# Experts' input rows fetched from DRAM by indirect DMA instead of being selected by matmuls

## The chip, the cores and the metric

The kernel runs on one core of one Trainium2 chip. The metric is the device time of one execution in microseconds (us). The core has TensorE (PE; its weight loads are listed apart as PEld), VectorE (DVE), ScalarE (ACT), GpSimd (POOL) and SyncE (SP), which issues nearly all transfers; 16 DMA engines carry them. "L0" and "L1" below are the two layers of the model, "L312" and the like are lines of the kernel.

## What is computed

Two layers over 256 latent tokens and, in the first layer, 256 context tokens, of width 1024 in float32. Each layer has a mixer and then a mixture of 32 experts; each token goes to the two best experts of its best group. The mixers don't change here. The expert part, cut down:

```python
def hier_moe(h, wg_r, bg_r, we_r, be_r, w_gate, w_up, w_down):   # h: (T, 1024), T = 512 in L0, 256 in L1
    pg = softmax(h @ wg_r + bg_r); pg_top, g_idx = top_k(pg, 1)             # 4 groups
    le = take_along_axis((h @ we_r + be_r).reshape(t, 4, 8), g_idx)         # 8 experts of the group
    pe_top, e_local = top_k(softmax(le), 2)
    wts = pg_top * pe_top / sum(pe_top)
    ...                                                                     # sort tokens by expert into blocks
    xs = h[slot_tok]                                                        # a row per slot
    ys = (silu(xs @ w_gate[e]) * (xs @ w_up[e])) @ w_down[e]                # 1024x512, 1024x512, 512x1024
    return segment_sum(ys * slot_w, slot_tok)
```

## The kernel before, in words

**Stages.** The program runs the L0 mixer, the L0 output projection with the router, the L0 experts, the L1 mixer, the L1 projection with the router, and the L1 experts. A scheduler orders the instructions of each engine by priority and by a model of time; inside `moe` the order on PE is the order in which the code is written (`manual_schedule`).

**Router.** `out_proj` ends with x_sb, the residual rows, 128 tokens a tile (NT = 4 tiles in L0, 2 in L1). `done` then calls, for each tile, `ffn_logits` (transposes, 36 logits), `route_tile` (DVE: ranks and the selection `selb`; PE counts over it) and `ffn_split`, which makes the expert input `h2` as a high part `h2h` and a low part `h2l` (ACT, DVE and POOL), all kept in SBUF. `route_end` turns the counts into `pos`, the place of each token among its expert's slots.

**Experts.** Each expert has CAP = 64 slots; two experts make a unit (u0 to u15 a layer, and in L0 one more, uX, of a single expert, for tokens above 64: `extra_block`, between u2 and u3). For a group of four experts `group` makes `gt`, a 0/1 matrix of tokens by slots (DVE, L435), and `gather` multiplies `h2h` and `h2l` with it (L265): the transposed input rows `xT` of 256 slots, 8 chunks of 128 features, NT tiles, two parts each. On PE a step of the loop over units is

- `hidden(0)`: first expert, 8 chunks of gate (L312) and up (L313) products, with hooks after given chunks (scatters of the units before, `places`);
- of the unit before: `turn` (L331), four transposes of its hidden layer, which DVE copies (`aT`, L333), a block of the gather for the next group, and `down` (L347), the product with w_down, then `yh`, `yl` on ACT and DVE or POOL;
- a second block of the gather, with the weights per slot (L285) in every second step;
- `hidden(1)`: the second expert, with hooks.

`scatter` (L370, L371) adds a unit's weighted result to the tokens' rows: PE multiplies (`sc`), DVE scales (`tm`, L375), DVE and POOL add (`x_sb`, L376). Each chunk-3 and chunk-7 hook holds one. In u0 the gather for the second group stands between the two experts, and the gather of uX stands between `turn` and `down` of u1.

**Weights.** An expert's weights are 6 tiles of 1 MiB; SP issues the loads in the order in which units use them (`moe_weights`), each into the next of a ring of tiles: NW = 5 named w and NX = 5 (L0) or 9 (L1) named wx. A load waits until its tile's last reader is done. The w tiles come free during the projection, the wx tiles lie where the projection's buffers were and can be loaded when it ends. A gate or up load reads 4 rows, 8 KB in a row, for each partition; a down load reads two rows of 4 KB that lie apart (`"(c p) f -> p c f"`, L153).

Of the kernel before, what the change touches and what calls it, by code (L numbers as in the profile page):

```python
# [25 lines left out]
I32 = mybir.dt.int32  # L26
U8 = mybir.dt.uint8
# [5 lines left out]
D = 1024  # L33
# [5 lines left out]
NX = (5, 9)  # L39
NZ = (0, 0)  # L40
EXTRA = 3
HP = 300
# [16 lines left out]
class Trunk:  # L59
# [13 lines left out]
    def consts(self, pool):  # L73
# [175 lines left out]
    def gather(self, NT, h2h, h2l, gt, ne):  # L249

        nc = self.nc
        N = ne * CAP
        if ne == 1:
            xT = self.mp.tile([128, 8, CAP], F32, name="xT1")
        else:
            xT = self.mp.tile([128, 8, GRP * CAP], F32, name="xT", bufs=2)
        per = 512 // N

        def part(c0):
            ps = self.mps.tile([128, 512], F32, name="xg", bufs=1).rearrange("p (k n) -> p k n", k=per)  # L260
            for k in range(per):
                i = 0
                for t in range(NT):
                    for src in (h2h, h2l):
                        nc.tensor.matmul(ps[:, k], src[:, t, c0 + k, :], gt[t], start=(i == 0), stop=(i == 2 * NT - 1))  # L265
                        i += 1
            if self.slot_mods is None:
                nc.scalar.activation(xT[:, c0:c0 + per, :], ps, AF.Copy)
            else:
                A, B = self.slot_mods  # L270
                for k in range(per):
                    c = c0 + k
                    nc.vector.tensor_scalar(xT[:, c], ps[:, k], A[:, 0, c:c + 1], B[:, 0, c:c + 1], op0=OP.mult, op1=OP.add)  # L273

        return xT, [lambda c0=c0: part(c0) for c0 in range(0, 8, per)]

    def slot_weights(self, NT, gt, whl, M, cols):

        nc = self.nc
        R = whl.shape[2]  # L280
        n = len(cols)
        pw = self.mps.tile([128, 512], F32, name="mx", bufs=1).rearrange("p (n r) -> p n r", r=64)
        for i in range(n):
            for t in range(NT):
                nc.tensor.matmul(pw[:M, i, 0:R], gt[t][:, i * M:(i + 1) * M], whl[:, t, :], start=(t == 0), stop=(t == NT - 1))  # L285
        wl = self.mp.tile([128, 2, 64], F32, name="wl", bufs=2)
        nc.vector.tensor_copy(wl[:M, 0:n, 0:R], pw[:M, 0:n, 0:R])
        ws = self.mp.tile([128, 2], F32, name="ws", bufs=3)
        for i in range(n):
            for j, (a, b) in enumerate(cols[i]):  # L290
                r = slice(64 * j, 64 * j + 64)
                nc.vector.tensor_add(ws[r, i:i + 1], wl[r, i, a:a + 1], wl[r, i, b:b + 1])
        return [ws[:, i:i + 1] for i in range(n)]

    def unit(self, W, xT, slots, ws, posbc, NT, x_sb, mx5, last=False):
# [92 lines left out]
    def slot_mx5(self, S, mx5):  # L388
# [4 lines left out]
        m = self.mp.tile([128, 8, GRP * CAP], F32, name="xT", bufs=2)  # L393
        m = m.rearrange("p c n -> p (c n)")[:, :D]
# [29 lines left out]
    def moe(self, l, NT, h2h, h2l, pos, whl, counts, weights, first, posT, x_sb, mx5, early):  # L424
# [1713 lines left out]
```

## Time and profile before

| | |
|---|---|
| runs (3), median | 1825.58 us (1823.93 to 1826.13) |
| the profiled execution, its own time | 1826.54 us |
| its span, first to last instruction | 1824.5 us |
| busy, share of the span | PE 93%, PEld 54%, DVE 47%, ACT 24%, POOL 20% |
| HBM read over the span | 508.09 MB, 280 GB/s on average |

The share of busy time says little here: PE is listed as busy over 90% in both expert stages, and a matmul's end is modelled. The stages are read apart: the first gate product of L0 starts at 444.8 us, the last scatter ends at 999.8 us; in L1 it is 1348.1 us and the end of the span.

### The profile page before, as it was taken

What the parts mean: (1) busy time and instruction counts of PE and PEld (TensorE: products, weight loads), DVE (VectorE), ACT (ScalarE), POOL (GpSimd) and SP (SyncE); (2) the same over time, 40 slices, a digit from 0 to 9 for tenths busy, and PEclk for the clock granted to TensorE, in tenths of its full rate; (3) what the DMA queues carried; (4) which work ended last, traced back from release to release, by engine and by line L of the source; (5) the groups of instructions that cost most, each with busy time, mean ns of one, the idle gap of its engine ahead of it and who ended that gap; (6) DMA issues with size and microseconds to landing.
All of it is one profiled execution on the core that took longest, in us unless ns stands there. A gap on an engine that the chain in (4) does not pass through costs nothing. (4 is left out here: it accounts for less than half of the span.)

```text
span 1824.5 us, 22067 instructions
## 1 busy us (share of the span) xinstructions
PE 1693.6 (93%) x8722; PEld 982.8 (54%) x8722; DVE 856.5 (47%) x1624; ACT 430.2 (24%) x692; POOL 357.6 (20%) x315
## 2 busy tenths in 40 slices
PE   6999988987999999999988998899879999999997
PEld 4766677775454444444433776588643334434442
DVE  3336158776234434344344678776443332333222
ACT  2335244432101110111101654443410000000000
POOL 2102055232011212112122300232310110101010
PEclk9999999987989999999998899899969999999999
DMA  8655530334978999999995335600479999999996
GB/s 295 236 213 210 211 124 25 119 98 165 373 322 322 395 385 400 396 395 401 392 387 194 122 110 198 228 31 1 155 290 415 415 417 416 416 416 417 416 416 282
DMA packets 115674, 511.79 MB, mean 281 GB/s; under 512 B 16254, under 2 KB 26434, under 8 KB 77031
## 3 DMA queue, kind: packets, MB, share of 16 engines
q1 hardware_dynamic: 115564, 510.31, 71.4%
q8 instruction: 71, 1.16, 0.3%
q14 instruction: 39, 0.32, 0.0%
HBM read 508.09 MB, written 2.18 MB: 280 GB/s over the span
## 5 line engine op out<-in xcount | busy, mean ns | idle before, releaser
L313 PE MATMUL gu<-wx,xT 128*64 128x512 f32 x640 | 292.2, 600 | 1.3 <-DMA wx<-moe_w_up_in 1.0
L312 PE MATMUL gu<-w,xT 128*64 128x512 f32 x568 | 262.0, 603 | 0.0
L312 PE MATMUL gu<-wx,xT 128*64 128x512 f32 x472 | 215.9, 599 | 0.0
L347 PE MATMUL y<-wx,aT 128*64 128x512 f32 x648 | 179.9, 615 | 12.1 <-DVE aT L333 9.0
L313 PE MATMUL gu<-w,xT 128*64 128x512 f32 x400 | 183.2, 602 | 0.5 <-SPq L599 0.5
L376 POOL TENSOR_TENSOR x_sb<-x_sb,tm 128x512 f32<-128x512 f32 x64 | 98.9, 1546 | 390.1 <-DVE tm L375 390.1
L316 ACT ACTIVATE sg<-gu 64x512 f32<-64x512 f32 x65 | 38.5, 592 | 555.6 <-PE gu L313 555.6
L375 DVE TENSOR_TENSOR tm<-sc,mx 128x512 f32<-128x512 f32 x128 | 85.5, 688 | 155.5 <-PE sc L371 153.8
L312 PEld LDWEIGHTS gu<-w,xT 128*64 128x64 f32 x568 | 72.5, 138 | 121.6 <-issue 118.1
L347 PE MATMUL y<-w,aT 128*64 128x512 f32 x392 | 120.1, 610 | 10.2 <-DVE aT L333 7.6
L265 PE MATMUL xg<-gt,h2h 128*128 128x256 f32 (+1 forms) x416 | 116.6, 314 | 10.3 <-DVE xT L273 6.0
L121 DVE TENSOR_TENSOR wl<-w,wh 128x1024 fp32r<-128x1024 f32 (+1 forms) x62 | 80.0, 1290 | 93.3 <-ACT wh L120 92.5
L265 PE MATMUL xg<-gt,h2l 128*128 128x256 f32 (+1 forms) x416 | 109.9, 297 | 0.0
L313 PEld LDWEIGHTS gu<-wx,xT 128*64 128x64 f32 x640 | 81.8, 137 | 43.9 <-issue 24.4
L347 PEld LDWEIGHTS y<-wx,aT 128*64 128x64 f32 x648 | 54.5, 141 | 93.8 <-issue 74.5
L265 PEld LDWEIGHTS xg<-gt,h2h 128*128 128x128 f32 x416 | 85.7, 206 | 34.5 <-DVE tm L356 10.5
L120 ACT ACTIVATE wh<-w 128x1024 fp32r<-128x1024 f32 (+1 forms) x72 | 75.0, 1047 | 122.5 <-PE acc L130 91.1
L312 PEld LDWEIGHTS gu<-wx,xT 128*64 128x64 f32 x472 | 59.7, 136 | 77.7 <-issue 71.2
L129 PE MATMUL acc<-wl,hT 128*128 128x512 f32 (+1 forms) x240 | 94.8, 395 | 0.0
L128 PE MATMUL acc<-wh,hT 128*128 128x512 f32 (+1 forms) x240 | 92.8, 401 | 0.0
L130 PE MATMUL acc<-wh,hT 128*128 128x512 f32 (+1 forms) x240 | 92.5, 392 | 0.0
L370 PE MATMUL sc<-yh,S 128*128 128x512 f32 (+1 forms) x194 | 87.3, 450 | 4.9 <-DVE tm L375 3.1
(638 smaller groups left out, 3017.2 us busy)
## 6 DMA issues: line engine op xcount, KB each, us to landing
wx<-moe_w_down_in SPq DMA_DIRECT2D x81, 1024.0 KB, 10.5
wx<-moe_w_up_in SPq DMA_DIRECT2D x80, 1024.0 KB, 14.0
w<-moe_w_gate_in SPq DMA_DIRECT2D x71, 1024.0 KB, 7.5
wx<-moe_w_gate_in SPq DMA_DIRECT2D x59, 1024.0 KB, 15.0
w<-moe_w_up_in SPq DMA_DIRECT2D x50, 1024.0 KB, 9.9
w<-moe_w_down_in SPq DMA_DIRECT2D x49, 1024.0 KB, 10.4
w<-ada_w_in SPq DMA_DIRECT2D x48, 1024.0 KB, 6.7
w<-even_w_in_in SPq DMA_DIRECT2D x14, 1024.0 KB, 8.6
```

The source lines that it names most:

```text
L120: nc.scalar.activation(hv, src, AF.Copy)
L121: self.lo_eng[0].tensor_tensor(lv, src, f32(hv), op=OP.subtract)
L128: mm(ps, a[0], b[0], start=start, stop=False)
L129: mm(ps, a[0], b[1], start=False, stop=False)
L130: mm(ps, a[1], b[0], start=False, stop=stop)
L265: nc.tensor.matmul(ps[:, k], src[:, t, c0 + k, :], gt[t], start=(i == 0), stop=(i == 2 * NT - 1))
L312: nc.tensor.matmul(g, xs[:, c, :], G[c // 4][:, c % 4, :], start=(c == 0), stop=(c == 7))
L313: nc.tensor.matmul(v, xs[:, c, :], U[c // 4][:, c % 4, :], start=(c == 0), stop=(c == 7))
L347: nc.tensor.matmul(y[h][r], u["aT"][:, c, r], W()[j][2][cc][:, c % 2, 512 * h:512 * h + 512], start=(c == 0), stop=(c == 3))
L370: nc.tensor.matmul(p, s, yh[:M], start=True, stop=False)
L375: nc.vector.tensor_mul(tm, p, mx5[t // 2][:, 512 * h:512 * h + 512])
L376: (nc.gpsimd if h else nc.vector).tensor_add(xv, xv, tm)
```

## The change

Each layer gets a DRAM table `h2d` of the expert input rows, written tile by tile by DMAs from ACT's queue (`ffn_rows`; no high and low parts). Two columns with the token's number are put beside the routing weights (`whl`, 64 to 66 columns), so that the matmul which summed the weights per slot also gives each slot's token number (`slot_sums`). DVE turns it into an index, POOL issues an indirect DMA that fetches 128 rows of 4 KB (`slot_rows`) into one of two buffers, and PE transposes these rows in 8 pieces (`turned`): per unit instead of per group, with the index made at chunk 1 of `hidden(0)` of the unit before, the transposes at chunks 2 and 6 of its `hidden(1)`. The router's steps get priority RP, route before rows. The second-last and last chunk of the projection's last pass are set aside and multiplied at its end. NX becomes (8, 11). The rows of a down load become `(p c)`, one run of 8 KB per partition, with the transposes of `turn` taking every fourth column to match. The register with the number of overflow blocks, read by every engine, is loaded at the third unit instead of at the end.

```diff
-NX = (5, 9)
+NX = (8, 11)
+RP = 300
@@ down_loads
-                d = self.ins["moe_w_down"][l, e].rearrange("(c p) f -> p c f", p=128)
+                d = self.ins["moe_w_down"][l, e].rearrange("(p c) f -> p c f", c=4)
@@
-    def gather(self, NT, h2h, h2l, gt, ne):
...
-                for t in range(NT):
-                    for src in (h2h, h2l):
-                        nc.tensor.matmul(ps[:, k], src[:, t, c0 + k, :], gt[t], start=(i == 0), stop=(i == 2 * NT - 1))
...
+    def slot_sums(self, NT, gt, whl, M):
+        R = whl.shape[2]
+        wl = self.mp.tile([128, 66], F32, name="wl", bufs=2)[:M, 0:R]
+        pw = self.mps.tile([128, 512], F32, name="mx", bufs=1)[:M, 0:R]
+        for t in range(NT):
+            self.nc.tensor.matmul(pw, gt[t], whl[:, t, :], start=(t == 0), stop=(t == NT - 1))
+        self.nc.vector.tensor_copy(wl, pw)
+        return wl
+
+    def slot_rows(self, NT, ids, M):
+        nc = self.nc
+        ix = self.mp.tile([128, 1], U32, name="ix", bufs=3)
+        nc.vector.scalar_tensor_tensor(ix[:M], ids[:, 0:1], 1024.0, ids[:, 1:2], op0=OP.add, op1=OP.add)
+        self.xgn += 1
+        xg = self.xgs[self.xgn % 2]
+        nc.gpsimd.indirect_dma_start(xg[:M], None, self.h2d[:, :], bass.IndirectOffsetOnAxis(ap=ix[:M, 0:1], axis=0),
+                                     bounds_check=NT * 128 - 1, oob_is_err=False)
+        return xg
+
+    def turned(self, xg, M, xT, banks=("xg",)):
...
+            for k in range(4):
+                c = 4 * i + k
+                nc.tensor.transpose(ps[:, k, 0:M], xg()[:M, c * 128:c * 128 + 128], self.ident[:M, :M])
             if self.slot_mods is None:
-                nc.scalar.activation(xT[:, c0:c0 + per, :], ps, AF.Copy)
+                nc.scalar.activation(xT[:, 4 * i:4 * i + 4], ps[:, :, 0:M], AF.Copy)
...
@@ turn
-                nc.tensor.transpose(pt[:, c * M:(c + 1) * M], u["a"][:M, c * 128:(c + 1) * 128], self.ident[:M, :M])
+                nc.tensor.transpose(pt[:, c * M:(c + 1) * M], u["a"][:M, c:512:4], self.ident[:M, :M])
@@ moe
+                if k == 2:
+                    traced = len(nc.cur_bb.bb.instructions)
+                    with tc.high_priority(offset=100000):
+                        n_blk = nc.values_load(ov[1][0:1, 0:1], min_val=0, max_val=2 * T // CAP)
...
+                nxt = []
+                if k + 1 < len(units):
+                    q = units[k + 1][0]
+                    nxt = extra[0] if q is None else inputs(q)
                 if before:
-                    hidden(0, {3: [lambda: some(scat), before[1]], 7: [lambda: some(scat)]})
+                    hidden(0, {1: nxt[:1], 3: [lambda: some(scat), before[1]], 7: [lambda: some(scat)]})
                     before[2]()
-                    if extra and k == EXTRA - 1:
-                        some(extra[0], 9)
-                    if p is not None:
-                        some(gath)
                     some(scat, 9)
                     scat += before[3]()
...
-                    some(gath, 1 if p % 2 == 0 else 9)
                     lastp = [place] if k == len(units) - 1 else []
-                    hidden(1, {3: [lambda: some(scat)] + lastp, 7: [lambda: some(scat)]})
+                    hidden(1, {2: nxt[1:2], 3: [lambda: some(scat)] + lastp, 6: nxt[2:], 7: [lambda: some(scat)]})
@@ out_proj
+                if s == 0 and c in order[6:]:
+                    held.append((c, (ah, al), w))
+                    continue
...
-                    (nc.gpsimd if h else nc.vector).tensor_add(xv, xv, tm)
+                    nc.vector.tensor_add(xv, xv, tm)
@@
-    def ffn_split(self, l, t, x, r, A2, B2, h2h, h2l, pool):
+    def ffn_rows(self, l, t, x, r, A2, B2, pool):
...
+        h = pool.tile([128, 8, 128], F32, name="h2", bufs=2)
         if l == 1:
-            nc.scalar.activation(h2h[:, t], xc, AF.Copy, scale=r)
...
+            nc.scalar.activation(h, xc, AF.Copy, scale=r)
+        else:
+            nc.vector.scalar_tensor_tensor(h, xc, r, A2[t // 2], op0=OP.mult, op1=OP.mult)
+            nc.vector.tensor_add(h, h, B2[t // 2])
+        nc.scalar.dma_start(self.h2d[t * 128:t * 128 + 128], h.rearrange("p a b -> p (a b)"))
```

On PE, at the start of the L0 experts (pr: counts over tokens, gu: gate and up products, gt: the 0/1 matrices) there stands before

```order
L199 MATMUL pr<-r_selb,c_ones 128x32
L205 MATMUL mx<-c_ident,r_pos 32x128 x4
L265 MATMUL xg<-gt,h2h 128x256
L265 MATMUL xg<-gt,h2l 128x256
...
L312 MATMUL gu<-w,xT 64x512
L313 MATMUL gu<-w,xT 64x512
```

and now

```order
L207 MATMUL pr<-r_selb,c_ones 128x32
L213 MATMUL mx<-c_ident,r_pos 32x128 x4
L263 MATMUL mx<-r_whl,gt 128x2 x4
L288 MATMUL xg<-c_ident,xg_2847 128x128 x4
L288 MATMUL sc<-c_ident,xg_2847 128x128 x4
L329 MATMUL gu<-w,xT 64x512
L330 MATMUL gu<-w,xT 64x512
```

Where 64 selecting matmuls stood, 4 short ones give the token numbers and 8 transposes wait for the fetched rows.

On PE around the `down` product of an L0 unit (y: its result, aT: the turned hidden layer) there stands before

```order
L331 MATMUL mx<-c_ident,a 128x128 x4
L265 MATMUL xg<-gt,h2h 128x256
L265 MATMUL xg<-gt,h2l 128x256
...
L347 MATMUL y<-w,aT 64x512
L347 MATMUL y<-wx,aT 64x512
...
L265 MATMUL xg<-gt,h2h 128x256
L265 MATMUL xg<-gt,h2l 128x256
...
L312 MATMUL gu<-wx,xT 64x512
L313 MATMUL gu<-wx,xT 64x512
```

and now

```order
L348 MATMUL mx<-c_ident,a 128x128 x4
L364 MATMUL y<-w,aT 64x512 x16
L329 MATMUL gu<-wx,xT 64x512
L330 MATMUL gu<-wx,xT 64x512
...
L330 MATMUL gu<-wx,xT 64x512
L288 MATMUL xg<-c_ident,xg_2846 128x128 x4
L329 MATMUL gu<-wx,xT 64x512
```

The two blocks of 16 selecting matmuls on either side of `down` are gone; the transposes of the next unit's rows stand inside the second expert.

On DVE in the same stretch of an L0 unit, up to the copy that `down` waits for, there stands before

```order
L375 TENSOR_TENSOR tm<-sc,mx_1_2838 128x512
L317 TENSOR_TENSOR a<-sg,gu 64x512
L375 TENSOR_TENSOR tm<-sc,mx_1_2838 128x512
L376 TENSOR_TENSOR x_sb<-x_sb,tm 128x512
L333 COPY aT<-mx 128x512
```

and now

```order
L392 TENSOR_TENSOR tm<-sc,mx_1_2841 128x512
L334 TENSOR_TENSOR a<-sg,gu 64x512
L392 TENSOR_TENSOR tm<-sc,mx_1_2841 128x512
L393 TENSOR_TENSOR x_sb<-x_sb,tm 128x512
L350 COPY aT<-mx 128x512
```

Nothing moved: four operations on scattered rows and on the next hidden layer still stand ahead of aT. In the L0 router, where POOL made `h2l` and half of the residual adds, POOL now has no large operation; both rows' `h` multiplications still precede the last selection on DVE.

## Rows read from the trace of the kernel before

**Rows 1.** SP's longest wait by releaser, L0 (450:1000 us): total us, times, longest.

```profile
SPq L137 <- PE gu L313: 261.1, 61, 10.4
```

**Rows 2.** The same in L1 (1400:1800 us).

```profile
SPq L137 <- DMA wx<-moe_w_down_in: 55.9, 28, 2.2
```

**Rows 3.** L265 in L0: length, PE busy (count), PEld busy, PEclk, DMA share, GB/s.

```profile
444.70:1001.00 556.30, 72.07 (x514) 66.02 (x512) 0.98 0.91 362
```

**Rows 4.** The turn of u6; down of u6 and u14, PE's timeline: start us, us.

```profile
700.75 0.60 PE L331 MATMUL mx<-c_ident,a 128*128 128x128 f32 x4
701.11 0.36 PE L265 MATMUL xg<-gt,h2h 128*128 128x256 f32 x1
...
703.87 7.09 PE L347 MATMUL y<-w,aT 128*64 128x512 f32 x32 [0.61 <-DVE aT L333]
958.16 8.78 PE L347 MATMUL y<-wx,aT 128*64 128x512 f32 x32 [2.52 <-DVE aT L333]
```

**Rows 5.** As u14's down begins: PE, PEld, DVE, ACT, POOL busy, PEclk, DMA, GB/s.

```profile
958.10:960.00 1.90, 1.84 (x6) 0.61 (x8) 0.00 (x1) 0.00 (x0) 0.53 (x1) 0.54 0.99 407
```

**Rows 6.** Turns of u0, u2, uX, u3, u13, u14, u15 in L0, PE's timeline.

```profile
473.99 0.66 PE L331 MATMUL mx<-c_ident,a 128*128 128x128 f32 x4
548.77 0.60 PE L331 MATMUL mx<-c_ident,a 128*128 128x128 f32 x4
573.08 0.46 PE L331 MATMUL mx<-c_ident,a 64*128 64x64 f32 x4
605.70 0.66 PE L331 MATMUL mx<-c_ident,a 128*128 128x128 f32 x4
924.17 0.60 PE L331 MATMUL mx<-c_ident,a 128*128 128x128 f32 x4
955.04 0.60 PE L331 MATMUL mx<-c_ident,a 128*128 128x128 f32 x4
982.74 1.06 PE L331 MATMUL mx<-c_ident,a 128*128 128x128 f32 x4
```

**Rows 7.** The gather between the two experts of u0, PE's timeline.

```profile
451.78 1.08 PE L285 MATMUL mx<-r_whl,gt 128*128 128x64 f32 x8
...
459.53 0.64 PE L312 MATMUL gu<-w,xT 128*64 128x512 f32 x1
```

**Rows 8.** From router to first product in L0: DVE and PE timelines.

```profile
419.11 2.38 DVE L184 TENSOR_SCALAR r_ohg<-r_sg,r_rg 128x4 f32<-128x4 f32 x1
427.33 2.10 DVE L187 SCALAR_TENSOR_TENSOR r_selb<-r_rank,r_ohg 128x32 bf16<-128x32 f32 x1
430.85 0.56 PE L265 MATMUL xg<-gt,h2h 128*128 128x256 f32 x1
444.76 0.64 PE L312 MATMUL gu<-w,xT 128*64 128x512 f32 x1
```

**Rows 9.** The clock in that gather (columns: rows 5).

```profile
437.00:440.00 3.00, 2.31 (x11) 2.02 (x11) 2.80 (x14) 0.60 (x1) 0.00 (x0) 0.60 0.00 0
```

**Rows 10.** Transfers in L1: a stretch of gate and up loads, one of down loads.

```profile
DMA packets 812, 5.89 MB, mean 421 GB/s; under 512 B 93, under 2 KB 93, under 8 KB 93
DMA packets 643, 2.47 MB, mean 411 GB/s; under 512 B 41, under 2 KB 41, under 8 KB 643
```

**Rows 11.** L1's first experts and a later stretch (columns: rows 5).

```profile
1342.90:1353.40 10.50, 9.37 (x36) 5.27 (x38) 1.99 (x4) 0.00 (x0) 0.00 (x0) 0.62 0.14 56
1357.00:1400.00 43.00, 40.75 (x194) 16.54 (x193) 15.55 (x34) 3.21 (x6) 2.84 (x3) 0.96 0.95 384
1400.00:1500.00 100.00, 100.00 (x480) 39.92 (x478) 36.79 (x67) 9.19 (x15) 11.37 (x12) 1.00 1.02 417
```

**Rows 12.** L1's first weight loads into freed tiles, SP's timeline.

```profile
1353.10 0.89 SPq L137 DMA_DIRECT2D w<-moe_w_down_in  x2
```

**Rows 13.** Issue to landing: a load of 512 KB, and up loads in L1, 1400:1800.

```profile
x_sb<-x_lat SPq DMA_DIRECT2D x2, 512.0 KB, 3.5
wx<-moe_w_up_in SPq DMA_DIRECT2D x37, 1024.0 KB, 19.1
```

More of the change, by code (lines that the diff above doesn't have):

```diff
@@ L26 @@
 I32 = mybir.dt.int32
+U32 = mybir.dt.uint32
 U8 = mybir.dt.uint8
@@ L269, in part @@
             else:
                 A, B = self.slot_mods
[L271 to L277, printed above, removed]
-        nc = self.nc
[L280 to L293, printed above, removed]
@@ new lines, in part, with slot_weights @@
+                for k in range(4):
+                    c = 4 * i + k
+                    if k % 2:
+                        nc.scalar.activation(xT[:, c], ps[:, k, 0:M], AF.Identity, bias=B[:, 0, c:c + 1], scale=A[:, 0, c:c + 1])
+                    else:
+                        nc.vector.tensor_scalar(xT[:, c], ps[:, k, 0:M], A[:, 0, c:c + 1], B[:, 0, c:c + 1], op0=OP.mult,
+                                                op1=OP.add)
+        return [lambda: part(0), lambda: part(1)]
+    def slot_weights(self, wl, cols):
+        nc = self.nc
+        ws = self.mp.tile([128, 1], F32, name="ws", bufs=4)
+        for j, (a, b) in enumerate(cols):
+            r = slice(64 * j, 64 * j + 64)
+            nc.vector.tensor_add(ws[r], wl[r, a:a + 1], wl[r, b:b + 1])
+        return ws
@@ L422, in moe_weights, with moe @@
             next(self.ahead)
-    def moe(self, l, NT, h2h, h2l, pos, whl, counts, weights, first, posT, x_sb, mx5, early):
+    def moe(self, l, NT, pos, whl, counts, weights, first, posT, x_sb, mx5, early):
         nc, tc = self.nc, self.tc
@@ L453, in moe @@
         with tc.manual_schedule(engines={mybir.EngineType.PE}):
-            *parts, w0 = group(0)
-            for f in parts:
-                f()
+            with tc.high_priority(offset=RP):
+                group(0)
+                *parts, w0 = inputs(0, False, ("xg", "sc"))
+                for f in parts:
+                    f()
             weights()
@@ L513, in moe @@
         self.ecount = 0
-        self.overflow(l, NT, h2h, h2l, pos, whl, ov, first, x_sb, mx5)
+        self.overflow(l, NT, pos, whl, (ov[0], n_blk), first, x_sb, mx5)
     def overflow_list(self, NT, counts, pool):
@@ L579, in prepare @@
                 gt.append(x)
-            have["xT"], parts = self.gather(NT, h2h, h2l, gt, 1)
-            for f in parts:
-                f()
-            have["ws"], = self.slot_weights(NT, gt, w2, CAP, [[(0, 1)]])
+            pw = self.slot_sums(NT, gt, w2, CAP)
+            have["x"] = self.slot_rows(NT, pw[:, 2:4], CAP)
+            have["ws"] = self.slot_weights(pw, [(0, 1)])
+        have["xT"] = mp.tile([128, 8, CAP], F32, name="xT1")
+        parts = [index] + self.turned(lambda: have["x"], CAP, have["xT"])
         def places():
@@ L612, in overflow @@
                 nc.vector.tensor_copy(wc, wx[:, :, :, ds(i, 1)].rearrange("p t k o -> p t (k o)"))
-                parts, (hidden, places, turn, down) = self.extra_block(lambda: [W], pc, wc, NT, h2h, h2l, whl, x_sb, mx5)
-                parts[0]()
+                parts, (hidden, places, turn, down) = self.extra_block(lambda: [W], pc, wc, NT, whl, x_sb, mx5)
+                for f in parts:
+                    f()
                 hidden(0)
@@ L1219, in out_proj, with products @@
             order = [2 * k + i for k in W for i in range(2)]
+            held = []
+            def products(i, h, c, a, w):
+                if c == order[0]:
+                    ps[i, h] = psum.tile([128, 512], F32, name="acc", bufs=4)
+                self.mm3(ps[i, h], [x[:, 128 * i:128 * i + 128] for x in a], [x[:, 512 * h:512 * h + 512] for x in w],
+                         c == order[0], c == order[7])
             for c in order:
@@ L1239, in out_proj @@
                 for h in range(2):
+                    for x in held:
+                        products(i, h, *x)
                     tm = pool.tile([128, 512], F32, name="otm", bufs=2)
@@ L2094, in build @@
             K.slot_mods = K.ffc[1] if l else None
-            K.moe(l, NT, h2h, h2l, pos, whl, counts, lambda: K.route_weights(NT, lg, ohg, rank, whl, K.mp), 1 - l, posT, x_sb, mx5, (lambda: None) if l else K.odd_early)
+            K.moe(l, NT, pos, whl, counts, lambda: K.route_weights(NT, lg, ohg, rank, whl, K.mp), 1 - l, posT, x_sb, mx5, (lambda: None) if l else K.odd_early)
         wst.close()
```

132 lines of the change are left out of this document (70 added, 62 removed).

## The prediction

> **What bounds the kernel now.** The shares of the whole span mix stages, so I read the two expert stages apart, and in each first who releases the engine that issues the loads. In L0, SP's longest waits end with a gate or up product [rows 1]: a weight tile isn't free yet, so TensorE sets the pace. In L1 they end with a landing [rows 2], and the 16 DMA engines are full at 417 GB/s [rows 11]: there DMA sets it. The change takes work from PE and gives bytes to DMA. So the question for L0 is which of PE's work really ends something, for L1 what the new bytes cost.
>
> The obvious count is L265: the gather keeps PE busy for 72.07 us in L0 [rows 3]. I did not take that as the gain, because of what stands beside each block of it. After the turn of u6 the block starts at 701.11, `down` at 703.87, and `down` still waited 0.61 us for DVE's aT [rows 4]: 3.12 us from turn to down. After the turn of u14 no gather is left, and `down` starts 958.16 − 955.04 = 3.12 us later all the same, now with 2.52 us of waiting for aT [rows 4, 6]. The block between turn and down is free. DVE gets to the copy aT only after four operations on scattered rows and on the next hidden layer, and these stand in the same order after the change. [...] All three L0 units whose turn has no gather behind it (u2, u13, u14) wait 2.52 us, and their clock falls each time.
>
> [...]
>
> **L0, part by part.** *First product.* Before: 444.76 [rows 8]. Two DVE rows of the route took 2.38 and 2.10 us [rows 8] while POOL made h2l; with POOL empty I take 0.2 each like their neighbours, −4.1, and +0.7 for a residual add that DVE takes over: the first 0/1 matrix is ready some 3.4 us earlier, so at 430.85 − 3.4 = 427.5 where the first gather product stood [rows 8]. From there my estimate is 5 us for eight `gt` and the index on DVE (no row shows this chain), 3.5 for the fetch by the nearest row, a 512 KB load [rows 13], and 2 for the transposes and the copy. That is 438; the trace of before has no indirect DMA, and the last table write and the fetch share the DMA engines with eight prefetched tiles, so I take 440, with 436 and 446 as ends. [...]
>
> *Cold start.* The gather also warmed PE: it began at half rate (430.85), and the clock reached full within 437 to 440 (mean 0.60, so about 0.6 us of 3 at full [rows 9]), 8.5 us later. Now PE idles there, and the first products do those 8.5 us at half rate: +4.3.
>
> *To u0's turn.* Before, 473.99 − 444.76 = 29.2, of which 459.53 − 451.78 = 7.75 is the second group's gather and its sums [rows 6, 7]; both go, and the latter covers no wait of down. Left are 21.5. New: the sums of slots and tokens twice, four products each where eight took 1.08 [rows 7], 1.0; eight transposes, four of which take 701.11 − 700.75 = 0.36 [rows 4], 0.7. So the turn is at 440 + 21.5 + 4.3 + 1.0 + 0.7 = 467.5.
>
> *Units.* From u3 to u13, with gather, a unit took (924.17 − 605.70)/10 = 31.85 us. From u13 to u14, without any but with the 2.52 us gap and the half clock, 955.04 − 924.17 = 30.87 [rows 6]. This is the new unit's skeleton; on it go eight transposes (0.7) and one set of sums (0.5): **32.1**. A unit becomes 0.25 us longer, not 4 shorter. Then: u1 and u2, 531.7 (the extra unit's gather, which swelled this stretch, is gone); uX, before 573.08 − 548.77 = 24.31, with 1.2 for the same additions, 557.2; u3, 589.3; eleven more, 942.4; u15, before 982.74 − 955.04 = 27.70 [rows 6], unchanged, **970.1**. Before: 982.74. L0 gives **−12.6**. Against its DMA: 12 tiles of 1.049 MB at 421 GB/s [rows 10] are 29.9 us, a fetch of 0.524 MB at the rate of 4 KB packets, 411, adds 1.3: 31.2, under 32.1, so PE stays the bound, and three more tiles in the ring buy nothing. The 1.3 us hides under 0.9 us of slack a unit and under the lead of the ring.
>
> The scatters, `places`, x_sb adds on POOL and DVE stay. On POOL an index wait now stands ahead of the next adds; I cost that at nothing, as POOL was busy 20% of the span; if the fetch's issue held an add for 2 us, DVE's tm and with it aT would come later. The two set-aside chunks of the projection and the register load at the third unit keep their work; I cost both at nothing (bounds −1 to +1).
>
> **L1: DMA.** *Added bytes:* 16 fetches and 2 table tiles of 0.524 MB, 9.4 MB at 411 GB/s: **+23.0**; the tail behind the last load is not touched, so all of it counts. *Down loads:* a third of the 187 tiles (five lie ready as the stage begins) or 65 MB, now runs of 8 KB; gate and up loads move at 421, down loads at 411 [rows 10]: 65.4/0.411 − 65.4/0.421 = **−3.8**. Bound: nothing, if the rate hangs on something else, and then +3.8. *Holes:* between 1342.9 and 1353.4 DMA moved 56 GB/s, from the ninth wx tile's landing to the first freed tile at 1353.10 [rows 11, 12]: 10.5 × (1 − 56/417) = 9.1 us lost; from 1357 to 1400, at 384, 3.4 more [rows 11]. Two more tiles fill 5.0 us, table and first fetches 3.8, and the first product comes about 4 us earlier but begins cold: I count **−12**, with −5 and −12.5 as ends. PE has 4 us of slack a unit in L1, so its own cold gaps cost nothing. Sum **+7** (+6 to +18).
>
> **Sum.** The profiled execution took 1826.54. −12.6 + 7 gives 1820.9; it lies 1 us above the median, so **1820**.
>
> **Rivals.** (1) *The clock holds* through the new gaps: 14 × 1.7 = −24 on PE; DMA at 31.2 a unit then limits it to 14 × 0.9 = 13, beyond which only the lead of the ring gives more: 1797 to 1807. Against it: three falls in three. (2) *DVE copies aT sooner* and the 72 us are all gained, L0 then at DMA's pace: 1780 to 1797. The unchanged order on DVE speaks against it. (3) *Slower: the fetch blocks the stream.* If 128 scattered rows hold the queues as long as a lone 512 KB load takes to land (3.5 us [rows 13], and not 1.3), each of L1's 16 costs 2.2 more: +35, and L0 goes beyond PE's pace by 1.3 a unit, +20: 1855 to 1875; half of it gives 1838. It decides early: the forecast of −5.6 turns into slower by 3.7 as soon as a fetch costs 9.3/16 = 0.6 us above its bytes. For it: no row shows a gather; against it: 4 KB packets alone move at 411. (4) *The fetch comes late.* If it stood behind SP's backlog (19.1 us to landing in L1 [rows 13]) PE would wait at the transposes, which are planned some 19 us after the index: up to 3 us a unit where DMA bounds, 1830. [...] (5) *The change doesn't do what it says:* the down loads keep 411; 1824, inside the range.
>
> **How the numbers follow.** What a measurement can tell from no change is about 0.2%, 3.7 us. My forecast (0.60), 1810 to 1829: about two thirds of it is faster, the rest mostly within. Rival 1: 0.13; 2: 0.07; 3: 0.12; 4: 0.08. Faster: 0.38 + 0.13 + 0.07 = 0.58; within: 0.17 + 0.03 = 0.20; slower: 0.05 + 0.12 + 0.05 = 0.22. The range leaves out most of rival 2 and the dear half of rival 3: 1793 to 1842.
>
> **What will show it.** Right: turns of L0 units 32 us apart, each down waiting 2.5 us for aT with a clock near 0.55 behind it; u15's turn near 970; L1 at 417 to 420 GB/s without a hole, units 31.2 apart. Wrong: turns below 31 us apart (rivals 1, 2); a drop of GB/s around each fetch (3); PE waiting for xg (4); a first product after 446.

## The result

The changed kernel takes 1798.64 us (median of 4 runs, 1796.72 to 1799.60) against 1825.86 (4 runs): a ratio of 0.9851, interval 0.9834 to 0.9869, so 27 us or 1.5% faster. The forecast was 1820, range 1793 to 1842: the sign and the range held, and the gain that was forecast was a fifth of the one that came. The profiled execution took 1799.0 us, its span is 1797.2.

| stretch, us | before | after | forecast |
|---|---|---|---|
| start to first weight load into a wx tile, L0 | 408.39 | 397.62 | 408.4 |
| from there to the first L0 product | 36.37 | 31.24 | 31.6 |
| first product to turn of u0 | 29.23 | 26.90 | 27.5 |
| u0 to u2 (before: with uX's gather) | 74.78 | 60.48 | 64.2 |
| u2 to u3 | 56.93 | 55.88 | 57.6 |
| u3 to u14 (11 units) | 349.34 | 350.88 | 353.1 |
| u14 to u15 | 27.70 | 26.03 | 27.7 |
| turn of u15 to first wx load in L1 | 336.18 | 334.54 | as before |
| from there to the last turn | 486.31 | 491.44 | +7 |
| last turn to the end of the span | 19.27 | 22.19 | as before |

The turns of the L0 units in the profile after, PE's timeline (u0, u2, uX, u3, u13, u14, u15), answer to [rows 6]:

```profile
455.76 0.75 PE L348 MATMUL mx<-c_ident,a 128*128 128x128 f32 x4
516.24 0.63 PE L348 MATMUL mx<-c_ident,a 128*128 128x128 f32 x4
541.33 0.69 PE L348 MATMUL mx<-c_ident,a 64*128 64x64 f32 x4
572.12 0.75 PE L348 MATMUL mx<-c_ident,a 128*128 128x128 f32 x4
892.34 0.63 PE L348 MATMUL mx<-c_ident,a 128*128 128x128 f32 x4
923.00 0.63 PE L348 MATMUL mx<-c_ident,a 128*128 128x128 f32 x4
949.03 1.06 PE L348 MATMUL mx<-c_ident,a 128*128 128x128 f32 x4
```

From u3 to u14 a unit takes 31.90 us where it took 31.76: 72 us of PE's work in L0 were taken out, and the steady pace is unchanged. What L0 gained behind its first product came where the gather had covered little or no wait: before the turn of u0, and from u0 to u2, where the gather of uX stood. Turn and down of u9 and u10, same view (brackets: idle time before, and what ended it), answer to [rows 4]:

```profile
763.54 0.63 PE L348 MATMUL mx<-c_ident,a 128*128 128x128 f32 x4
766.65 8.78 PE L364 MATMUL y<-wx,aT 128*64 128x512 f32 x32 [2.48 <-DVE aT L350]
...
796.58 0.63 PE L348 MATMUL mx<-c_ident,a 128*128 128x128 f32 x4
799.70 7.09 PE L364 MATMUL y<-wx,aT 128*64 128x512 f32 x32 [2.48 <-DVE aT L350]
```

Turn to down is 3.11 or 3.12 us in both, as in u6 and u14 before; what the gather filled of it is now waiting. It is so in 14 of the 17 units of L0 (u1, u2 and u3 to u14; u3 has 3.03). But only u9 has the long down. The granted clock as the two downs begin (columns as in [rows 5]):

```profile
766.70:768.60 1.90, 1.90 (x8) 0.60 (x10) 0.00 (x0) 0.00 (x0) 0.43 (x1) 0.69 1.01 418
799.70:801.60 1.90, 1.90 (x10) 0.76 (x12) 0.00 (x0) 0.00 (x0) 0.47 (x1) 1.00 1.01 410
```

Between 572 and 892 four units of ten lose the clock and take 33.0 us, the other six 31.35; of the 14 gaps of 2.3 to 2.5 us in L0 these four are the only ones with a long down behind them (u3, u6, u9, u11). Summed, PE waited in L0 (430:960):

```profile
PE y L364 <- DVE aT L350: 36.1, 16, 2.5
```

The start of L0, DVE, POOL and PE timelines, answers to [rows 8]:

```profile
414.10 0.23 DVE L192 TENSOR_SCALAR r_ohg<-r_sg,r_rg 128x4 f32<-128x4 f32 x1
...
423.23 1.25 POOL L275 DMA_INDIRECT xg<-h2d,ix  x1 [8.70 <-DVE r_m L231]
...
426.96 1.12 PE L288 MATMUL xg<-c_ident,xg 128*128 128x128 f32 x4 [7.13 <-DMA xg<-h2d,ix]
...
428.86 1.12 PE L329 MATMUL gu<-w,xT 128*64 128x512 f32 x1
...
433.24 0.64 PE L329 MATMUL gu<-w,xT 128*64 128x512 f32 x1
```

The selection isn't stretched any more (0.23 for 2.38), the fetch lands 3.7 us after its start, and the first products run at half rate for 4.4 us (mean granted clock 0.54 from 428.80 to 433.24, 1.00 from there to 436).

The first weight load goes out 10.8 us earlier and the first product comes 15.9 earlier. To see where, I take a mark that the load does not move: the projection works in two passes of two tiles each, and each ends with DVE's `otm`, the scaled result. The first `otm` of each pass, before and after, DVE's timeline:

```profile
367.02 1.29 DVE L1241 TENSOR_TENSOR otm<-acc,mx 128x512 f32<-128x512 f32 x2 [0.35 <-PE acc L130]
407.04 1.29 DVE L1241 TENSOR_TENSOR otm<-acc,mx 128x512 f32<-128x512 f32 x2 [2.14 <-PE acc L130]
```

```profile
367.11 1.29 DVE L1301 TENSOR_TENSOR otm<-acc,mx 128x512 f32<-128x512 f32 x2 [0.35 <-PE acc L138]
399.36 1.29 DVE L1301 TENSOR_TENSOR otm<-acc,mx 128x512 f32<-128x512 f32 x2 [2.14 <-PE acc L138]
```

The first pass ends at the same time. The second takes 7.8 us less (32.25 for 40.02), and from its end to the first product it is 8.2 less (29.50 for 37.72). The remaining 3.1 of the load's 10.8 are the load's own: it goes out 1.74 us ahead of that second mark, where it stood 1.35 behind it.

The second pass in the kernel before, POOL's and DVE's timelines: POOL's addition to h and its h2l, and on DVE the next tile's h and the split of the projection's weights.

```profile
377.36 3.90 POOL L1302 TENSOR_TENSOR h<-h,B 128x1024 f32<-128x1024 f32 x1 [2.43 <-DVE nr L626]
382.43 3.67 POOL L1304 TENSOR_TENSOR h2l<-h,h2h 128x1024 fp32r<-128x1024 f32 x1 [0.66 <-ACT h2h L1303]
...
381.81 2.14 DVE L1301 SCALAR_TENSOR_TENSOR h<-x_sb,nr,A 128x1024 f32<-128x1024 f32 x1 [2.81 <-POOL nr L627]
384.00 3.18 DVE L121 TENSOR_TENSOR wl<-w,wh 128x1024 fp32r<-128x1024 f32 x1
```

PE's longest wait there (us in total, times, longest):

```profile
PE acc L129 <- DVE wl L121: 4.3, 1, 4.3
```

The stretch as a whole (columns as in [rows 5]):

```profile
380.00:400.00 20.00, 14.52 (x55) 11.92 (x54) 16.99 (x30) 5.89 (x9) 8.42 (x4) 0.74 0.33 105
```

After, the same wait:

```profile
PE acc L137 <- DVE wl L129: 1.5, 1, 1.5
```

and the same stretch:

```profile
380.00:400.00 20.00, 18.15 (x93) 14.59 (x92) 17.08 (x40) 6.40 (x9) 0.00 (x0) 1.00 0.46 151
```

L0's router works on its first two tiles while the projection still multiplies for the last two. POOL's long operations hold DVE up in two ways here. DVE stands idle for 2.81 us until POOL has made the small `nr`, which lies behind POOL's addition of 3.90 us. And POOL's 3.67 us of h2l lie beside a DVE operation that takes 3.18 where the same line takes 1.2 elsewhere. PE waits 4.3 us for it, and the mean clock of the stretch is 0.74. After, POOL is idle (0.00), and the clock full (1.00).

L1's start after, POOL and PE timelines: a POOL operation behind the table's write, the first fetch, the first transposes.

```profile
1310.78 0.28 POOL L483 CAST sr<-c_ident 32x128 fp32r<-32x128 f32 x1 [14.42 <-DMA h2d<-h]
1311.62 1.11 POOL L275 DMA_INDIRECT xg<-h2d,ix  x1 [0.56 <-issue]
1319.38 1.12 PE L288 MATMUL xg<-c_ident,xg 128*128 128x128 f32 x4 [18.62 <-DMA xg<-h2d,ix]
```

Two stretches of L1 after (columns as in [rows 5]), beside [rows 11]:

```profile
1318.00:1328.00 10.00, 8.62 (x34) 3.84 (x36) 2.15 (x8) 3.00 (x5) 1.00 (x1) 0.71 0.08 16
1400.00:1500.00 100.00, 96.87 (x439) 34.73 (x435) 32.98 (x66) 15.57 (x29) 14.08 (x14) 1.00 1.01 420
```

POOL waits 14.42 us for the table's write, PE 18.62 for the fetch behind it: both lie in the stream of prefetched tiles. The first product comes 37.7 us after the first wx load (before: 29.2), and the hole of 10 us stays although two more tiles are fetched ahead. The load moved against the projection here too: it goes out 0.4 us ahead of the projection's end (first `otm` at 1283.98), where it stood 1.4 behind it (1317.55). From that end to the last turn L1 takes 3.3 us more, not 5.1, and the 1.6 that the table shows between u15 and the load are this shift and no gain. And the page's DMA queues (packets, MB, share):

```profile
q0 software_dynamic: 4688, 6.30, 1.0%
q10 hardware_dynamic: 864, 3.15, 0.4%
```

q10 are the table writes, six of 0.524 MB. q0 are the fetches: 6.30 MB, where 33 fetches of all their rows (128, and 64 for uX) would be 17. An empty slot's index lies out of bounds, and its row isn't moved (17.04 MB with every index in bounds, e5).

### The profile page after: what moved, and what is told of

The parts are those of the page before. It is cut to its first block, busy times and chain, and to the rows that moved or that the text cites. A ratio compares the mean times of both kernels' runs of the same rounds, so it can differ in the third digit from the quotient of the medians.

```text
span 1797.2 us, 21195 instructions
## 1 busy us (share of the span) xinstructions
PE 1620.4 (90%) x8160; PEld 878.7 (49%) x8160; DVE 855.2 (48%) x1685; ACT 455.1 (25%) x753; POOL 363.6 (20%) x340
## 3 DMA queue, kind: packets, MB, share of 16 engines
q0 software_dynamic: 4688, 6.30, 1.0%
HBM read 525.13 MB, written 5.33 MB: 295 GB/s over the span
## 5 line engine op out<-in xcount | busy, mean ns | idle before, releaser
L330 PE MATMUL gu<-wx,xT 128*64 128x512 f32 x704 | 332.7, 602 | 2.8 <-DMA wx<-moe_w_up_in 2.4
L329 PE MATMUL gu<-wx,xT 128*64 128x512 f32 x616 | 291.3, 601 | 0.0
L364 PE MATMUL y<-wx,aT 128*64 128x512 f32 x696 | 191.1, 613 | 39.2 <-DVE aT L350 33.4
L329 PE MATMUL gu<-w,xT 128*64 128x512 f32 x424 | 204.6, 609 | 0.0
L330 PE MATMUL gu<-w,xT 128*64 128x512 f32 x336 | 161.5, 611 | 0.9 <-DMA w<-moe_w_up_in 0.9
L329 PEld LDWEIGHTS gu<-wx,xT 128*64 128x64 f32 x616 | 74.9, 136 | 109.2 <-issue 105.9
L364 PEld LDWEIGHTS y<-wx,aT 128*64 128x64 f32 x696 | 59.8, 140 | 140.0 <-issue 88.0
L364 PE MATMUL y<-w,aT 128*64 128x512 f32 x344 | 104.0, 619 | 15.9 <-DVE aT L350 15.2
L330 PEld LDWEIGHTS gu<-wx,xT 128*64 128x64 f32 x704 | 85.3, 136 | 40.0 <-issue 31.7
L329 PEld LDWEIGHTS gu<-w,xT 128*64 128x64 f32 x424 | 52.0, 138 | 71.7 <-issue 68.6
L376 POOL TENSOR_TENSOR yl<-tm,yh 128x512 fp32r<-128x512 f32 x30 | 38.1, 1270 | 210.6 <-ACT yh L375 210.6
L275 POOL DMA_INDIRECT xg<-h2d,ix x33 | 33.9, 1026 | 229.3 <-DVE ws L309 186.1
L298 DVE TENSOR_SCALAR xT<-xg,f1A,f1B 128x128 f32<-128x128 f32 x62 | 25.4, 410 | 114.8 <-PE xg L288 99.0
```

The lines of the kernel that those rows point to most:

```text
L329: nc.tensor.matmul(g, xs[:, c, :], G[c // 4][:, c % 4, :], start=(c == 0), stop=(c == 7))
L330: nc.tensor.matmul(v, xs[:, c, :], U[c // 4][:, c % 4, :], start=(c == 0), stop=(c == 7))
L364: nc.tensor.matmul(y[h][r], u["aT"][:, c, r], W()[j][2][cc][:, c % 2, 512 * h:512 * h + 512], start=(c == 0), stop=(c == 3))
```

## The experiments

Theory A: POOL's long operations stretched DVE's, and that held the projection and the route (the way up to the first product). Theory B: the gap between turn and down belongs to DVE's queue ahead of aT; it took what the gather's removal gave in L0. Rivals: the projection's other edits for A, PE's own work for B. Differences of medians are to the changed kernel's 1798.64 or to the kernel before in the same series (1826.74 for e1 to e4, 1825.84 for e5 to e8, 1825.03 for e9 to e11; 1825.86 beside the changed kernel). For e1, e6, e8, e9, e10 and e11 the interval of the ratio to the kernel before overlaps that of the changed kernel (0.9834 to 0.9869), so their medians alone show no difference from it; there the stretches of one profile each carry the argument. The profiles reach the end of the projection's first pass anywhere between 363.8 and 370.3 us, in code that all share, so the start of L0 is compared from there:

| us | before | e2 | e1 | after | e8 |
|---|---|---|---|---|---|
| end of the first pass to end of the second (first `otm` of each) | 40.02 | 33.94 | 35.23 | 32.25 | 32.26 |
| from there to the first wx load | 1.35 | 1.35 | −1.74 | −1.74 | 1.38 |
| from there to the first product | 37.72 | 34.25 | 32.61 | 29.50 | 29.43 |

The other variants of the kernel before (e4, e7) have 39.6 and 38.6 in the first row and 35.9 and 37.6 in the last, the other variants of the changed kernel 31.9 to 32.3 and 29.4 to 30.5.

**e1: POOL gets a long operation again.**

```diff
+        h2x = pool.tile([128, 8, 128], BF, name="h2x")
+        nc.gpsimd.tensor_tensor(h2x, h, h, op=OP.subtract)
```

> The changed kernel with one useless POOL operation a router tile (h minus h, 128x1024, into a scratch tile), as large as the one that made h2l. Theory A (POOL's long operations stretched DVE's wl split by 2 us and more, PE waited and lost its clock, so the projection ended 8 to 11 us later): the first L0 product comes 6 to 10 us after the 428.9 of the changed kernel, the time rises by 6 to 10 us to 1805 to 1809. Rival (the earlier projection comes from the two set-aside chunks or the residual adds): first product within 2 us of 428.9, time within 2 us of 1798.6.

1804.49 us (1802.70 to 1806.73), 5.9 more than the changed kernel and just under what was expected. The first product is at 431.66, only 2.8 later, and the first wx load at 397.31, no later; but this profile reached the end of the first pass 3.3 us earlier. Counted from there the second pass takes 3.0 us more and the route 3.1, so the product comes 6.1 later, within the 6 to 10 expected. POOL and DVE timelines of e1:

```profile
374.69 1.89 POOL L1360 TENSOR_TENSOR h2x<-h 128x1024 bf16<-128x1024 f32 x1
...
374.75 3.66 DVE L1356 SCALAR_TENSOR_TENSOR h<-x_sb,nr,A 128x1024 f32<-128x1024 f32 x1 [0.45 <-POOL nr L676]
...
415.27 1.86 DVE L192 TENSOR_SCALAR r_ohg<-r_sg,r_rg 128x4 f32<-128x4 f32 x1
```

The stretching is there (3.66 for 2.2, 1.86 for 0.22), although this operation took 1.9 us, half of h2l's 3.67. The stretched h stands on DVE ahead of the weights' split, and PE's wait for that split is 3.0 us instead of 1.5. So a POOL operation that nothing waits for costs the start of L0 some 6 us. (This profile also has two more clock falls than the changed kernel's, 3.3 us; in the variants with aT on DVE and nothing in the gap there are four to six, so differences of 3 us in L0 can be that.)

**e2: the kernel before, with these POOL operations on DVE.**

```diff
-        (nc.vector if t % 2 else nc.gpsimd).tensor_add(h, h, B2[t // 2])
+        nc.vector.tensor_add(h, h, B2[t // 2])
-        nc.gpsimd.tensor_tensor(h2l[:, t], h, f32(h2h[:, t]), op=OP.subtract)
+        nc.vector.tensor_tensor(h2l[:, t], h, f32(h2h[:, t]), op=OP.subtract)
```

> The kernel before, with the L0 router's h addition and h2l subtraction on DVE instead of POOL and nothing else. Theory A: the longest wl row before the last projection pass (3.18 us) falls to 1.2, the first weight load into a wx tile moves from 408.4 to 400 to 403, the first product from 444.8 to 437 to 441, the time falls by 4 to 8 us to 1818 to 1822. Rival (the projection's other edits did it): load at 406 to 410, time within 2 us of 1825.9 or later, as DVE has 6 us more to do.

1820.54 us (ratio 0.9973, 0.9957 to 0.9989): 6.2 less. First wx load 400.66 (408.39 before), first product 433.56 (444.76), earlier still than expected. DVE has more to do, and the load and the product are 8 and 11 us earlier, of which 1.7 lie in the code that all share. The stretch of the projection in e2:

```profile
380.00:400.00 20.00, 18.00 (x88) 14.56 (x89) 18.17 (x40) 7.35 (x10) 0.00 (x0) 1.00 0.39 125
```

POOL 0.00, clock 1.00, as in the changed kernel. Theory A holds for the kernel before in so far as it was POOL's two operations that held the start of L0: without them the second pass takes 6.1 us less of the 7.8 that the change brought, and the route is 34.3 us, 1.7 to 3.5 below the three profiles with them, of 8.2. Every split of weights in this stretch takes 1.2 us, and DVE waits 0.45 for the second tile's `nr`. But e2 takes away both ways of holding DVE up at once, so how much each cost in the kernel before isn't shown. In e1, where DVE waits no longer for `nr` than in e2, the stretching alone is left.

**e3: aT copied by ACT, in the changed kernel.**

```diff
-            nc.vector.tensor_copy(aT, pt[:, :4 * M].rearrange("p (c m) -> p c m", c=4))
+            nc.scalar.activation(aT, pt[:, :4 * M].rearrange("p (c m) -> p c m", c=4), AF.Copy)
```

> The changed kernel with the copy aT on ACT instead of DVE. Theory B (the gap between turn and down is DVE's queue ahead of aT, and takes what the gather's removal gave): turn to down falls from 3.1 us to 1.3 to 1.6 in L0, no clock fall behind it, units from 31.9 us to 29.5 to 30.6, where DMA takes over; L0 gains 18 to 30 us, L1 nothing (DMA-bound): 1769 to 1782. Rival (the gap is PE's own, turn's result is late anyway): gap 2.8 to 3.1, time within 3 us of 1798.6.

**1766.71 us** (1764.74 to 1768.85), ratio 0.9681 (0.9649 to 0.9712): 32 us below the changed kernel, 2 below the range expected, and the fastest version here. PE's timeline of e3, a turn and its down:

```profile
686.12 0.63 PE L348 MATMUL mx<-c_ident,a 128*128 128x128 f32 x4
687.44 3.65 PE L364 MATMUL y<-wx,aT 128*64 128x512 f32 x16 [0.69 <-ACT aT L350]
```

The stretch from 600 to 900 us of e3 (columns as in [rows 5]),

```profile
600.00:900.00 300.00, 293.13 (x1312) 112.69 (x1310) 135.46 (x219) 44.17 (x71) 72.69 (x59) 1.00 1.01 420
```

and of the changed kernel:

```profile
600.00:900.00 300.00, 275.20 (x1209) 105.61 (x1210) 134.63 (x219) 34.36 (x55) 69.31 (x57) 0.98 0.99 403
```

The gap is 1.32 us, no clock falls, and units from u5 to u13 take 29.56 us, each 1.79 less than 31.35, as much as the gap shrank. 14 gaps of 1.79 and the four falls of 1.69 make 31.8 us, and from the first wx load to the turn of u15 e3 takes 519.5 us, 31.9 less than the changed kernel. Theory B holds. DMA moves 420 GB/s, as in L1, but has not taken over as the expectation had it: from 430 to 930 us PE waits for no weight tile, only for aT (11.0 us in 16 waits) and for the results to be scattered.

**e4: aT copied by ACT, in the kernel before** (the same edit).

> The kernel before with the copy aT on ACT. Theory B: there the gather block of 2.1 us covers the gap, so only the 0.6 us of waiting a unit behind the block and the 1.5 to 2 us with three clock falls in the units without one go: 12 to 16 us less at most, L0 then at 31.1 us a unit with the gather, 1812 to 1820. So the change is worth 27 us with aT on DVE and 35 to 45 with aT on ACT. Rival (the gather costs nothing in PE wherever aT is): both fall by the same amount.

1814.84 us (1810.20 to 1815.50): 11.9 less. Units from u4 to u13 alternate between 30.77 and 31.61 us. So with aT on ACT the change is worth 1814.84 − 1766.71 = 48 us (a little over the 35 to 45 expected), with aT on DVE 27: some 20 us of its worth lie behind DVE's queue.

**e9: the gap filled with useless PE work.**

```diff
                     before[2]()
+                    if first:
+                        fl = self.mps.tile([128, 512], F32, name="xg", bufs=1)
+                        for i in range(16):
+                            nc.tensor.transpose(fl[:, 128 * (i % 4):128 * (i % 4) + 128], self.ident, self.ident)
```

> The changed kernel with 16 useless transposes of the identity on PE between turn and down in L0 (some 1.6 us in the gap of 2.5, nothing reads them). If the clock falls because PE stands idle in the gap: no unit of 33.0 us is left, all are 31.35, about 5 falls x 1.7 us less, -5 to -9 us: 1790 to 1794, although PE does more. If the falls have another cause: 33.0 stays in about a third of the units, time within 2 us of 1798.6. If the filler itself delays down: units above 31.6.

1795.45 us (1791.93 to 1797.28): 3.2 less with more work, a little short of the range expected; every unit from u3 to u13 takes 31.27 to 31.35, none 33.0. First wx load to turn of u15 is 546.4 us instead of 551.4: four falls of 1.7 less, against 0.9 more each behind the turns of u0 and uX, where the filler covers little or no wait. A turn with filler and down, PE's timeline of e9:

```profile
699.95 0.63 PE L348 MATMUL mx<-c_ident,a 128*128 128x128 f32 x4
700.42 1.91 PE L543 MATMUL xg<-c_ident 128*128 128x128 f32 x16
703.07 3.65 PE L364 MATMUL y<-wx,aT 128*64 128x512 f32 x16 [0.74 <-DVE aT L350]
```

So here the idle gap is what costs the clock, in the four units where it does (33.0 us for 31.35), and the wait itself is DVE's: down starts 3.12 us after the turn with or without work between.

**e5: empty slots fetch row 0.**

```diff
-        nc.gpsimd.iota(self.tid[:, :, 1], pattern=[[128, 4]], base=-1024, channel_multiplier=0,
+        nc.gpsimd.iota(self.tid[:, :, 1], pattern=[[128, 4]], base=0, channel_multiplier=0,
-        nc.vector.scalar_tensor_tensor(ix[:M], ids[:, 0:1], 1024.0, ids[:, 1:2], op0=OP.add, op1=OP.add)
+        nc.vector.scalar_tensor_tensor(ix[:M], ids[:, 0:1], 0.0, ids[:, 1:2], op0=OP.add, op1=OP.add)
```

> The changed kernel, but an empty slot's index is 0 and not out of bounds, so every fetch brings all 128 rows: 17.3 MB instead of 6.3 MB, in L1 8.4 instead of 2.1 MB. If the forecast's +23 us for L1 was wrong only because empty slots aren't fetched: +6.3 MB at 411 GB/s, +15 us in L1 and nothing in L0, where PE sets the pace: 1812 to 1816. If a fetch's bytes are hidden anyway: within 3 us of 1798.6. If fetches disturb the stream beyond their bytes: above 1818.

1812.28 us (1810.74 to 1818.18): 13.6 more than the changed kernel, as expected. In e5 the page's queue row reads

```profile
q0 software_dynamic: 4688, 17.04, 2.5%
```

The same 4688 packets, 17.04 MB for 6.30. First wx load to last turn in L1 is 502.2 us, not 491.4: 10.7 more, less than the 15 expected, and the first product is only 0.5 of it. L0 keeps its 31.35 and 33.0; its 3.9 us more are two more clock falls (3.3) and a first product 1.0 later. So the bytes of a fetch are paid where DMA bounds, but by less than 6.3 MB at 411 GB/s. Against the kernel before e5's stretch is 15.9 longer, and the forecast's terms, with the slow stretch of [rows 11] gone but nothing won at the hole, are +23.0 − 3.8 − 3.4 = 15.8: with every row moved, the term for bytes comes out, and the changed kernel pays some 4.6 us more than for the rows it moves. That the skipped rows cost this is possible and not shown: their packets, of 4 bytes, took about 1 us of the 16 engines in L1.

**e6 and e7: the down loads in runs of 4 KB in the changed kernel, of 8 KB in the kernel before** (the two lines of the diff at `down_loads` and `turn`, undone or done alone).

> The changed kernel with the down loads as before (two runs of 4 KB a partition). L1 is bound by DMA: 65 MB at 411 instead of 421 GB/s, +3 to +5 us, 1802 to 1804, L0 unchanged; L1's stretch 1400 to 1700 falls from 420 to 416 GB/s. Rival (the higher rate is the other traffic's): within 1.5 us of 1798.6.

> The kernel before with the down loads as runs of 8 KB and nothing else. L1 at 420 GB/s from 1520 us on, where it is bound by DMA: -3 to -4 us, 1821.5 to 1823. Rival: within 1.5 us of 1825.9.

e6: 1801.20 (1799.42 to 1803.99), 2.6 more. e7: 1820.74 (1816.48 to 1825.15), ratio 0.9974 (0.9961 to 0.9987), 5.1 less. L1's windows from 1600 to 1700 us (columns as in [rows 5]) of the changed kernel and of e6:

```profile
1600.00:1700.00 100.00, 91.51 (x381) 33.20 (x383) 28.00 (x56) 12.81 (x24) 11.50 (x12) 1.00 1.01 419
```

```profile
1600.00:1700.00 100.00, 91.53 (x383) 33.64 (x381) 28.23 (x56) 13.40 (x25) 11.52 (x12) 0.98 1.02 416
```

419 to 416, and 417 to 420 in e7; from the first wx load to the last turn of L1 e7 takes 482.5 us, 3.8 less than the kernel before, just the term. In e6 that stretch is only 1.0 us longer than in the changed kernel; the first product comes 1.6 sooner there, and from it on the units take about 0.26 more each where DMA bounds, 2.6 in all.

**e8: the rings of before** (NX back to (5, 9)).

> The changed kernel with the rings of before, NX (5, 9). In L0 PE sets the pace: within 2 us there, if the hole at the first experts doesn't grow by more than 3 tiles x 2.5 us, which PE would see one unit later. In L1 the backlog ends 5 us sooner, so the table write and the first fetch land sooner and the first product too, and the hole of 10 us stays as long: 0 to +4 us. Sum 1797 to 1804. Rival (the ring's two tiles in L1 are 5 us saved at the DMA-bound end, as the forecast counted): 1803 to 1808.

1802.61 us (1795.97 to 1805.58). First load to last turn in L1 takes 491.3 us with and without the added tiles. But the old rings put the first load 3.1 us later against the projection in L0 (table above) and 1.8 later in L1, as in the kernel before; why a tile of the old ring comes free later isn't shown. Counted from the projection's end L0's first product comes at the same time (29.4 us, 29.5 with), and L0 is 3.1 us longer up to the turn of u15, of which two more clock falls are 3.4. In L1 the first product is 4.3 us sooner, the last turn 1.6 later. So the five added tiles bring nothing in L0, where PE bounds, and about 1.6 us in L1, by the earlier start; there they also lengthen the backlog ahead of the first fetch.

**e10 and e11: the route's priority (RP = 0) and the two set-aside chunks, undone.**

> The changed kernel with RP = 0: the index of the first rows stands behind other small DVE work again. First L0 product 1 to 3 us later, the same in L1 at most (there the table write is late anyway): 1799 to 1803. Rival (the priority is what made the route short): first product 5 us later and more, 1804 to 1808.

> The changed kernel without the two set-aside chunks. The order on PE is the same with and without, so: within 2 us of 1798.6. If it were what shortened the projection: first weight load into a wx tile at 404 and later instead of 397 to 402, 1804 to 1810.

e10: 1800.17 (1796.60 to 1801.43), first product 31.4 us after the first wx load (31.2 with): the priority is worth nothing that can be seen. e11: 1798.41 (1796.63 to 1802.58), first wx load at 396.02, and the second pass takes 32.28 us (32.25 with): the set-aside chunks are not what shortened the projection.

## Why the prediction was right, and where its size was off

**Right: the gather between turn and down was free.** The 3.12 us of [rows 4] stand in 14 of the 17 L0 units after, with 2.48 us of waiting. e3 and e4 show whose gap it is. Whoever had booked the 72 us of [rows 3] would have been far off: from the projection's end to the turn of u15 the change took 26 us out of L0 (575.7 to 549.7), and e3 58.

**The term that failed: the start of L0.** The forecast has −3.4 us from the two stretched rows of [rows 8] and, with the shorter fetch chain, a first product 4.8 us earlier; it left the projection where it was. The product came 15.9 earlier. The projection's second pass gave 7.8 of it, of which e2 brings 6.1 by POOL's two operations alone; what brought the other 1.7 (the residual adds taken off POOL, or the new order of route and rows) was not run alone. The route from there gave 8.2, 3.4 more than forecast. That the stretch from the first wx load to the product came out as forecast (31.24 us for 31.6) is luck: the load itself had moved by 3.1. These 11 us are half of the 21 that the forecast missed. POOL's operations were in the forecast as a cause, but only with the rows between the router and the first product; the step that failed is that it charged them nothing in the projection.

How POOL's operation holds up DVE's isn't shown. `wl` started at 384.00, beside POOL's h2l (382.43, 3.67 us), and ended at 387.18, 1.1 us after POOL's 386.10, about its own length of 1.2: as if it had run once POOL was done. But beside POOL's addition (377.36) the same line took 1.22, at 377.44, and there it was POOL's that was long: 3.90, where the same line takes 2.36 at 415.29. DVE's 2.81 us of waiting for `nr` are another matter: a small operation stood behind a long one on POOL.

**Two terms off, with opposite signs.** A unit: the forecast put its additions at 1.2 us and a clock fall in each, 32.1. Without a fall a unit takes 31.35; the skeleton without fall is 30.87 − 1.69 = 29.18, so the additions cost 2.2. The trace shows where, in a unit after (PE's timeline, a block of four transposes between two chunks):

```profile
847.26 0.59 PE L329 MATMUL gu<-w,xT 128*64 128x512 f32 x1
847.79 0.65 PE L288 MATMUL xg<-c_ident,xg 128*128 128x128 f32 x4
848.38 0.64 PE L329 MATMUL gu<-w,xT 128*64 128x512 f32 x1
```

The next chunk starts 1.12 us after the last, where chunks without a block between them are 0.43 apart: four transposes cost 0.7 there and not 0.36, the time from the start of a turn to the next instruction that the forecast had read from [rows 4]. Eight cost 1.4 to 1.5 for 0.7, the sums, read the same way, 0.7 for 0.5. The falls come in four of the ten units between 572 and 892. The mean, 31.90, lies near the forecast because the two errors cancel: that is luck. What decides which gap loses the clock stays open: the gaps are equally long, and in e11, with the same order on PE, the falls stand behind u3, u6, u8 and u11 instead of u3, u6, u9 and u11.

**Smaller ones.** The cold start cost 4.4 us at half rate (0.54), 2.2, not 4.3. From u0 to u2 the forecast charged falls that did not come (29.53 and 30.95 us), −3.7 against it; u15 took 1.7 less for the same reason. From the turn of u0 to that of u15 the units came 9.3 us shorter than forecast, most of the other half of what it missed.

**L1: +5.1 for a forecast of +7, by terms that were wrong.** The +23.0 for bytes counted full fetches; 2.1 MB of filled rows and 1.05 MB of table are 7.7 us. The −12 for the holes did not come: the first product was not 4 us earlier but 8.5 later (6.7 counted from the projection's end), behind the backlog that the larger ring itself makes. That is rival 4, at one place instead of in each unit. The −3.8 for the down loads was right (e7). With the slow stretch from 1357 to 1400 [rows 11], gone after, −3.4, the measured terms give +0.5: that +5.1 lies so near +7 is luck, and 4.6 us of the +5.1 are not assigned (e5 bears on them). 1.8 us of earlier start, which only the rings of the changed kernel have, stand against it. The 2.9 us more after the last turn are no clear effect: the first transfer of the output is issued 2.7 us after DVE's last addition instead of 0.3, but 0.1 after it in e3, and this last stretch is 19.6 to 23.7 us in the profiles of the changed kernel's variants and 19.3 to 21.3 in those of the kernel before.

**Rivals.** Rival 3 fell: in L1 the stream stays at 419 to 420 GB/s with fetches in it, and full fetches (e5) cost no more than their bytes. Rival 2 is e3, not the change. Rival 1 was true of ten of the 14 gaps of 2.3 to 2.5 us, and the time lies within its range, but by the start of L0 as much as by the clock. Its 1.7 us a fall is the difference of the two downs of [rows 4], 8.78 − 7.09, and u9 and u10 after show the same 1.69; its three falls in three are granted clocks of 0.55, 0.56 and 0.54 [rows 5] in the first 1.9 us of down of u2, u13 and u14 before; after, four of the 14 gaps had a fall.

## What to carry to other kernels

Before work is taken off the busiest engine, look at what that engine waits for right behind it: if the wait ends at the same time with and without the work, as it showed in three units of the trace before (3.11 to 3.12 us from turn to down, as with the gather), the work is free, and the gain lies in the wait, here one line that gives a copy to an idle engine. And when a change empties an engine, search all the time in which it was busy for slow neighbours (here 3.18 us for 1.2) and for small operations queued behind long ones (2.81 us of waiting), not only the stretch that the change is about. Measure a stretch from a mark that the change does not move: the first weight load was none. The prefetch that ran ahead of a dependent small transfer delayed it here: with two more tiles ahead of it, L1's first product came 4.3 us later (e8).

## What the runs showed of the hardware beyond that

Rows whose index is out of bounds were skipped: the same 4688 packets, 6.30 MB instead of 17.04 (e5). Yet the HBM read on the page of the profile rose from 508.09 to 525.13 MB in the changed kernel already, by the 17 MB of full fetches, so that figure doesn't tell moved bytes here.

In L1 the table's write (q10, from ACT's queue) ran beside the prefetched loads (q1). The DMA queues from 1304 to 1310 us of the changed kernel:

```profile
q1 hardware_dynamic: 237, 1.78, 70.7%
q10 hardware_dynamic: 211, 0.75, 30.6%
```

In these 6 us the write got 30.6% of the engines beside the loads' 70.7%, with about as many packets, 211 and 237, and half as many bytes a packet (3.6 and 7.5 KB on average); how an engine chooses between queues isn't shown. The two tiles, 1.05 MB, took 12 us, issued from 1298.3 us on and landed by 1310.8.
